# Window attention that divides by the softmax sum at the end instead of scaling the probabilities, with transfers that carry the sums and the halves of the result

## The chip, the cores and the metric

The kernel runs on 1 core of one Trainium2 chip. A core has a matrix engine (TensorE, PE in the profile; PEld are its weight loads), a vector engine (VectorE, DVE), an activation engine (ScalarE, ACT), a general engine (GpSimd, POOL) and an engine that issues transfers (SyncE, SP). Each runs its own list of instructions in order. They meet only at semaphores. The metric is the device time of one launch in microseconds (us). The time before is 2276.86 us, the median of 3 runs (2275.3 to 2279.8).

## The reference

The program is a trunk of two layers for 1024 tokens of width 1024, in float32. Layer 0 has two recurrences side by side (RG-LRU and HGRN2), layer 1 has windowed attention, and each is followed by a squared-ReLU MLP. Only the attention is touched. Its core is:

```python
q = rope(q.reshape(bsz, s, N_Q_HEADS, HEAD_DIM), cos, sin)       # 16 query heads of 64
k = rope(k.reshape(bsz, s, N_KV_HEADS, HEAD_DIM), cos, sin)      # 4 key heads, 4 query heads share one
sc = jnp.einsum('bnqhgd,bnkhd->bnhgqk', qb, kb).astype(jnp.float32) * (HEAD_DIM ** -0.5)
sc = jnp.where(band_mask[None, :, None, None], sc, -jnp.inf)     # +-128 tokens: blocks n-1, n, n+1
sink = jnp.broadcast_to(sinks..., sc.shape[:-1] + (1,))          # one more logit per head
p = jax.nn.softmax(jnp.concatenate([sc, sink], axis=-1), axis=-1)[..., :-1]
o = jnp.einsum('bnhgqk,bnkhd->bnqhgd', p.astype(vb.dtype), vb)
return o.reshape(bsz, s, N_Q_HEADS * HEAD_DIM) @ w_o
```

The sink is a logit that takes part in the softmax's maximum and sum and has no value row.

## The kernel before, in words

Matrix products keep float32 accuracy by splitting an operand into a rounded part (`hi`) and a rest (`lo`), each a matmul operand; `split` (L84 to L86) makes `hi` on ScalarE and `lo` on VectorE or, in the attention, for weights, on GpSimd.

The attention has two kinds of work. A **slab** is one projection of 128 output columns for half of the tokens: 24 matmuls (`proj`, L116), a copy out (L1074), four transfers that swap halves for the rotary positions (L1076), and rotary arithmetic on VectorE (L1077) and GpSimd (L1078, L1079). Weights of a slab come by one transfer of 512 KB into a tile with the tag `raw` (two buffers, L90) and are then split. A **unit** is one key head g (four query heads) and one block n of 128 queries; there are 32 units (`U00` to `U37`). A unit does this:

- for each of four heads, the scores: two matmuls (L1150, L1151), then one VectorE instruction that adds the mask, stores the 384 scores (256 at the ends) to `sm` and gives the row maximum `mx` (L1153);
- `nm`, the negative maximum with the sink (L1157), the sink's own exponential `es` (L1159, L1160), then four exponentials with their row sums `den` (L1163, ScalarE);
- `den` plus `es` (L1164), its reciprocal (L1165), and four VectorE instructions that scale the probabilities of a head by it (L1167);
- for each of 3 (or 2) key blocks: four transposes into one PSUM bank (L1172), the `hi`/`lo` split `ph`/`pl` (L85, L86), two matmuls with the values (L1177, L1178). The value operand holds `hi` in columns 0 to 63 and `lo` in 64 to 127, so the result `po` has two halves of 64 partitions that have to be added;
- the upper half is copied to `posb` (L1180, ScalarE) and four VectorE instructions add it to the lower half in PSUM and write 64x128 pieces of the result rows `ys` (L1183).

The order of slabs and units is written out in the string `ATT_ORDER`; a `!` marks a unit issued at high priority. A scheduler then merges all into one list per engine, by priorities, dependences and its own model of durations. So an edit in a unit moves the order of the whole stage. After the last unit the output projection (L216) multiplies `ys` by `w_o`, first for the rows of key heads 0 and 1, which may start while units run.

Of the kernel before, what the change touches and what calls it, by code (L numbers as in the profile page):

```python
# [18 lines left out]
P = 128  # L19
# [32 lines left out]
def trunk_kernel(ctx, tc, x, norm_g, rec_w_in, rec_conv_w, rec_conv_b, rg_w_r, rg_b_r, rg_w_i,  # L52
# [997 lines left out]
    def attention(xt, a):  # L1050
        w_qkv = att_w_qkv[a]
        ys = [yp.tile([P, S], F32, tag="y", name=f"y{i}") for i in range(KT)]
        with phase("att") as pool:
# [12 lines left out]

            def h512(name, bufs=2):
                return pool.tile([P, 512], F32, tag=name, name=name, bufs=bufs)
# [71 lines left out]
            def unit(g, n):  # L1140
# [4 lines left out]
                mx = pool.tile([P, GRP], F32, tag="mx", name="mx", bufs=2)  # L1145
                sm = []
                for j in range(GRP):
# [4 lines left out]
                    s_ = pool.tile([P, nk * P], F32, tag="sm", name="sm", bufs=8)  # L1152
                    V.tensor_tensor_reduce(out=s_, in0=o, in1=mask[:, mo:mo + nk * P], scale=1.0, scalar=-1e30,  # L1153
                                           op0=ALU.add, op1=ALU.max, accum_out=mx[:, j:j + 1])
                    sm.append(s_)
                nm = pool.tile([P, GRP], F32, tag="nm", name="nm", bufs=2)
                V.scalar_tensor_tensor(nm, mx, -0.125, nsink[:, g * GRP:(g + 1) * GRP], op0=ALU.mult, op1=ALU.min)  # L1157
                es = pool.tile([P, GRP], F32, tag="es", name="es", bufs=1)
                V.tensor_tensor(es, sink[:, g * GRP:(g + 1) * GRP], nm, op=ALU.add)  # L1159
                A.activation(es, es, AF.Exp)  # L1160
                den = pool.tile([P, GRP], F32, tag="den", name="den", bufs=2)
                for j in range(GRP):
                    A.activation(sm[j], sm[j], AF.Exp, scale=0.125, bias=nm[:, j:j + 1], accum_out=den[:, j:j + 1])  # L1163
                V.tensor_tensor(den, den, es, op=ALU.add)  # L1164
                V.reciprocal(den, den)  # L1165
                for j in range(GRP):
                    V.tensor_scalar(sm[j], sm[j], den[:, j:j + 1], None, op0=ALU.mult)  # L1167
                po = mm_ps("aux")
                for kc in range(nk):
                    pt = mm_ps("aux")  # L1170
                    for j in range(GRP):
                        T.transpose(pt[:, j * P:(j + 1) * P], sm[j][:, kc * P:(kc + 1) * P], ident)  # L1172
# [6 lines left out]
                ph_ = pool.tile([64, 512], F32, tag="po", name="posb", bufs=1)  # L1179
                A.activation(ph_, po[64:128, :], AF.Copy)  # L1180
                for j in range(GRP):
                    dst = ys[2 * g + j // 2][64 * (j % 2):64 * (j % 2) + 64, n * P:(n + 1) * P]
                    V.tensor_tensor(dst, po[0:64, j * P:(j + 1) * P], ph_[:, j * P:(j + 1) * P], op=ALU.add)  # L1183
# [114 lines left out]
```

## Time and profile before

| | |
|---|---|
| median of 3 runs | 2276.86 us (2275.3 to 2279.8) |
| the profiled execution, its own time | 2277.96 us |
| its span | 2276.3 us |
| TensorE busy | 2169.1 us, 95% of the span |
| VectorE busy | 1724.0 us, 76% |
| ScalarE busy | 1143.6 us, 50% |
| GpSimd busy | 251.0 us, 11% |
| scores of the first unit to values of the last | about 1247 to 1560 us of the span |

The share of an engine is an average over stages that have different limits; the attention is one of them, some 14% of the span. In the groups of the profile a row names line, engine, operation, output <- input, shape and count, then the busy time of the group and the mean duration of one. "Idle" behind the bar is the time in which the engine did nothing just before such an instruction, with what ended it.

### The profile page before, as it was taken

To read this page: it belongs to the slowest core of one execution; us is meant where nothing else is said; L and a number is where in the kernel's file an instruction comes from. 1 tells how busy PE (TensorE), PEld (TensorE's weight loads), DVE (VectorE), ACT (ScalarE), POOL (GpSimd) and SP (SyncE) were. 2 spreads that over 40 slices of the span, in tenths; PEclk is the share of its full clock that TensorE was granted. 3 is DMA by queue.
4 is the path that set the end of the run, shared out by engine and by line. 5 is a ranking of instruction groups with operands and counts; after the bars stand their busy time and mean duration, and the time that the engine had idled before them with its cause. 6 is when DMAs were issued, how large, how long until landed. Compare 5 with 4: busy or idle time off the path is not lost. (4 is left out here: it accounts for less than half of the span.)

```text
span 2276.3 us, 28192 instructions
## 1 busy us (share of the span) xinstructions
PE 2169.1 (95%) x10392; PEld 1785.3 (78%) x10392; DVE 1724.0 (76%) x2930; ACT 1143.6 (50%) x1812; POOL 251.0 (11%) x139
## 2 busy tenths in 40 slices
PE   7999999899899999999999888989899999999998
PEld 6878888687688888888888766668678888888886
DVE  6597766757966665678887888996986666578887
ACT  5576545445544445433434666775554445533342
POOL 1131000103000000000023244320300000000003
PEclk9999999999999999999999999999999999999999
DMA  5111001034344447444434111114444443644433
GB/s 140 51 33 56 29 29 37 28 104 148 120 166 153 153 144 254 153 139 150 138 124 141 46 38 44 40 38 139 139 138 151 152 152 135 249 139 153 153 117 129
DMA packets 180763, 264.03 MB, mean 116 GB/s; under 512 B 17040, under 2 KB 98960, under 8 KB 180624
## 3 DMA queue, kind: packets, MB, share of 16 engines
q1 hardware_dynamic: 180624, 262.22, 35.1%
q8 instruction: 82, 1.34, 0.2%
q14 instruction: 57, 0.47, 0.1%
HBM read 179.87 MB, written 70.78 MB: 110 GB/s over the span
## 5 line engine op out<-in xcount | busy, mean ns | idle before, releaser
L116 PE MATMUL m<-xh,w1hl 128*128 128x512 f32 (+1 forms) x1472 | 429.9, 371 | 0.2 <-ACT qf L1074 0.2
L116 PEld LDWEIGHTS m<-xh,w1hl 128*128 128x128 f32 x1472 | 266.9, 192 | 38.0 <-ACT qf L1074 0.4
L116 PE MATMUL m<-xl,w1hl 128*128 128x512 f32 (+1 forms) x736 | 274.0, 372 | 0.0
L236 POOL TENSOR_TENSOR mg<-acc,g 128x1024 f32<-128x1024 f32 x32 | 83.5, 2610 | 1447.3 <-DVE acc L553 1207.3
L86 DVE TENSOR_TENSOR w1hl<-raw,w1hl 128x1024 fp32r<-128x1024 f32 x105 | 132.1, 1260 | 100.0 <-ACT w1hl L85 99.7
L418 PE MATMUL aux<-xh,w1hl 128*128 128x512 f32 x512 | 168.3, 390 | 0.0
L418 PE MATMUL m<-xh,w1hl 128*128 128x512 f32 x512 | 168.0, 390 | 0.4 <-ACT xh L85 0.4
L418 PE MATMUL m<-xh,ws 128*128 128x512 f32 x512 | 167.8, 390 | 0.0
L567 ACT ACTIVATE hidh<-hidl 128x1536 fp32r<-128x1536 f32 (+1 forms) x56 | 89.4, 1597 | 147.9 <-DMA hidl<-hs 147.9
L644 PE MATMUL m<-w2h,hidh 128*128 128x512 f32 x416 | 161.8, 389 | 0.0
L644 PE MATMUL m<-w2l,hidh 128*128 128x512 f32 x416 | 161.8, 389 | 0.0
L644 PE MATMUL m<-w2h,hidl 128*128 128x512 f32 x416 | 161.8, 389 | 0.0
L116 PEld LDWEIGHTS m<-xl,w1hl 128*128 128x128 f32 x736 | 141.8, 193 | 19.1 <-DVE xl L205 0.2
L568 DVE TENSOR_TENSOR hidl<-hidl,hidh 128x1536 fp32r<-128x1536 f32 (+1 forms) x56 | 105.9, 1891 | 56.9 <-ACT hidh L567 56.9
L85 ACT ACTIVATE w1hl<-raw 128x1024 fp32r<-128x1024 f32 x116 | 122.2, 1055 | 32.0 <-PE m L418 11.0
L85 ACT ACTIVATE ws<-s 128x512 fp32r<-128x512 f32 x88 | 55.4, 632 | 145.2 <-PE m L418 88.0
L85 ACT ACTIVATE w2h<-b 128x1536 fp32r<-128x1536 f32 (+1 forms) x48 | 76.7, 1598 | 100.4 <-PE m L644 49.1
L644 PE MATMUL aux<-w2h,hidh 128*128 128x512 f32 x312 | 121.4, 389 | 0.0
L644 PE MATMUL aux<-w2l,hidh 128*128 128x512 f32 x312 | 121.4, 389 | 0.0
L644 PE MATMUL aux<-w2h,hidl 128*128 128x512 f32 x312 | 121.4, 389 | 0.0
L418 PEld LDWEIGHTS m<-xh,w1hl 128*128 128x128 f32 x512 | 96.2, 188 | 21.0 <-ACT xh L85 1.2
L418 PEld LDWEIGHTS m<-xh,ws 128*128 128x128 f32 x512 | 96.1, 188 | 20.9 <-ACT ws L85 0.6
(298 smaller groups left out, 5165.9 us busy)
## 6 DMA issues: line engine op xcount, KB each, us to landing
hidl<-hs SPq DMA_DIRECT2D x42, 768.0 KB, 4.6
raw<-in_mlp_w_dram SPq DMA_DIRECT2D x30, 1024.0 KB, 5.5
hs<-hid SPq DMA_DIRECT2D x104, 256.0 KB, 2.1
b<-in_mlp_w_dram SPq DMA_DIRECT2D x24, 768.0 KB, 4.8
raw<-in_rec_w_in_dram SPq DMA_DIRECT2D x28, 512.0 KB, 3.8
hidl<-hs SPq DMA_DIRECT2D x14, 1024.0 KB, 5.6
hs<-u SPq DMA_DIRECT2D x52, 256.0 KB, 2.0
hres<-hb SPq DMA_DIRECT2D x24, 512.0 KB, 3.1
```

Of the source, the lines that this page charges most:

```text
L85: A.activation(hi, src, AF.Copy)
L86: (eng or V).tensor_tensor(lo, src, hi, op=ALU.subtract)
L116: T.matmul(o[:, c0:c0 + nw], a[:, k, :], b[k // 4][half][:, k % 4, c0:c0 + nw], start=(n == 0), stop=(n == 3 * KT - 1))
L236: G.tensor_tensor(mg, m, g_post, op=ALU.mult)
L418: T.matmul(o, a[:, k, :], b[:, k, :], start=(first and n == 0), stop=(n == 11), skip_group_check=not first)
L567: A.activation(h, f32(l), AF.Copy)
L568: V.tensor_tensor(l, f32(l), h, op=ALU.subtract)
L644: T.matmul(o, a_[:, j, sl], b_[:, j, :], start=(not more and n == 0), stop=(n == last), skip_group_check=more)
```

## The change

- The probabilities are no longer scaled. The reciprocal sums `den` (128 queries x 4 heads) are stored to DRAM as 4 rows of 128 numbers, and each row is read back broadcast over 64 partitions, into `rd`.
- The result `po` is copied out whole (128 partitions). Two transfers move its halves to the other partitions (64 x 256 numbers each), so that heads of even number have their rest on partitions 0 to 63 and heads of odd number on 64 to 127. Two VectorE instructions (64x256) add, two (128x128) multiply by `rd` and write `ys`.
- The sink is column 0 of the score tile: GpSimd copies `nsink` there, the exponential covers one column more and its row sum holds the sink. Scores are stored times -0.125, the running minimum starts at `nsink`, so `nm`, `es` and the addition to `den` need no instructions of their own.
- The scratch tiles `x_` and `rd` (two sets) live in one of the two `raw` buffers for the whole attention. The score tile is one tile of four heads with two buffers, where there were eight of one head.

```diff
+            scr = wp.tile([P, 2, 2, 2, P], F32, tag="raw", name="scr")
+            scr = [(scr[:, i, 0], scr[:, i, 1]) for i in range(2)]
...
-                mx = pool.tile([P, GRP], F32, tag="mx", name="mx", bufs=2)
-                sm = []
+                nm = pool.tile([P, GRP], F32, tag="nm", name="nm", bufs=2)
+                sm = pool.tile([P, GRP, 3 * P + 1], F32, tag="sm", name="sm", bufs=2)
+                heads = slice(g * GRP, (g + 1) * GRP)
+                G.tensor_copy(sm[:, :, 0:1], nsink[:, heads].rearrange("p (j o) -> p j o", o=1))
                 for j in range(GRP):
...
-                    s_ = pool.tile([P, nk * P], F32, tag="sm", name="sm", bufs=8)
-                    V.tensor_tensor_reduce(out=s_, in0=o, in1=mask[:, mo:mo + nk * P], scale=1.0, scalar=-1e30,
-                                           op0=ALU.add, op1=ALU.max, accum_out=mx[:, j:j + 1])
-                    sm.append(s_)
-                nm = pool.tile([P, GRP], F32, tag="nm", name="nm", bufs=2)
-                V.scalar_tensor_tensor(nm, mx, -0.125, nsink[:, g * GRP:(g + 1) * GRP], op0=ALU.mult, op1=ALU.min)
-                es = pool.tile([P, GRP], F32, tag="es", name="es", bufs=1)
-                V.tensor_tensor(es, sink[:, g * GRP:(g + 1) * GRP], nm, op=ALU.add)
-                A.activation(es, es, AF.Exp)
+                    V.tensor_tensor_reduce(out=sm[:, j, 1:1 + nk * P], in0=o, in1=mask[:, mo:mo + nk * P], scale=-0.125,
+                                           scalar=nsink[:, g * GRP + j:g * GRP + j + 1], op0=ALU.add, op1=ALU.min,
+                                           accum_out=nm[:, j:j + 1])
                 den = pool.tile([P, GRP], F32, tag="den", name="den", bufs=2)
                 for j in range(GRP):
-                    A.activation(sm[j], sm[j], AF.Exp, scale=0.125, bias=nm[:, j:j + 1], accum_out=den[:, j:j + 1])
-                V.tensor_tensor(den, den, es, op=ALU.add)
+                    e_ = sm[:, j, 0:1 + nk * P]
+                    A.activation(e_, e_, AF.Exp, scale=-1.0, bias=nm[:, j:j + 1], accum_out=den[:, j:j + 1])
                 V.reciprocal(den, den)
-                for j in range(GRP):
-                    V.tensor_scalar(sm[j], sm[j], den[:, j:j + 1], None, op0=ALU.mult)
+                den_d = dr.tile([GRP, P], F32, name=f"den{a}_{g}{n}")
+                Y.dma_start(den_d.rearrange("j q -> q j"), den)
                 po = mm_ps("aux")
...
-                ph_ = pool.tile([64, 512], F32, tag="po", name="posb", bufs=1)
-                A.activation(ph_, po[64:128, :], AF.Copy)
-                for j in range(GRP):
-                    dst = ys[2 * g + j // 2][64 * (j % 2):64 * (j % 2) + 64, n * P:(n + 1) * P]
-                    V.tensor_tensor(dst, po[0:64, j * P:(j + 1) * P], ph_[:, j * P:(j + 1) * P], op=ALU.add)
+                t = h512("po", 1)
+                A.activation(t, po, AF.Copy)
+                t4 = t.rearrange("p (j e q) -> p j e q", j=2, e=2)
+                x_, rd = scr[n % 2]
+                for e in range(2):
+                    dst, src = slice(64 * e, 64 * e + 64), slice(64 - 64 * e, 128 - 64 * e)
+                    Y.dma_start(x_[dst], t4[src, :, e, :])
+                    Y.dma_start(rd[dst], den_d.rearrange("(j e) q -> e j q", e=2)[e].partition_broadcast(64))
+                    V.tensor_tensor(x_[dst], t4[dst, :, e, :], x_[dst], op=ALU.add)
+                for j in range(2):
+                    V.tensor_tensor(ys[2 * g + j][:, n * P:(n + 1) * P], x_[:, j], rd[:, j], op=ALU.mult)
```

The scheduler gives other lists on each engine from about the attention on. Three places follow. Lines of the changed kernel are shifted: L1157 there is the score instruction, L1163 the exponential, L1164 the reciprocal, L1166 the store of `den`, L1179 the copy of `po`, L1184 the transfers of its halves into `scr`, L1185 the reads of `den` into `scr`, L1186 and L1188 the additions and products, L1151 the copy of the sink. Names of waits are the engine, or one of eight counters of transfers, that a row waits for.

VectorE, the end of a unit's softmax in the second half of the attention, before:

```order
L1164 TENSOR_TENSOR den<-den,es 128x4 [waits Activation_49]
L86 TENSOR_TENSOR pl<-aux,ph 128x512 [waits Activation_49]
L1157 SCALAR_TENSOR_TENSOR nm<-mx,nsink 128x4 [waits DVE_49]
L1165 RECIPROCAL den<-den 128x4 [waits DVE_49]
L1183 TENSOR_TENSOR y_9689<-aux,posb 64x128
L1159 TENSOR_TENSOR es<-sink,nm 128x4 [waits DVE_49]
L1167 TENSOR_SCALAR sm<-sm,den 128x384 [waits DVE_49]
L1167 TENSOR_SCALAR sm<-sm,den 128x384 x3
```

and VectorE behind the reciprocal of one of the last units of key head 1, in the change:

```order
L1164 RECIPROCAL den<-den 128x4 [waits DMAHW5_49,Activation_49]
L86 TENSOR_TENSOR pl<-aux,ph 128x512 [waits Activation_49]
L1080 TENSOR_TENSOR qf<-qf,cos 128x512 [waits DMAHW6_49,DMAHW5_49,DMAHW7_49,DMAHW0_49,Pool_49]
L1186 TENSOR_TENSOR scr<-po,scr 64x256 [waits DMAHW1_49]
L86 TENSOR_TENSOR pl<-aux,ph 128x512 [waits Activation_49]
L1186 TENSOR_TENSOR scr<-po,scr 64x256 [waits DMAHW2_49]
L86 TENSOR_TENSOR pl<-aux,ph 128x512 [waits Activation_49]
L1188 TENSOR_TENSOR y_9684<-scr 128x128 [waits DVE_49]
```

The scaling between reciprocal and transposes is gone; additions that wait for a transfer now stand between the splits `pl`, for which TensorE waits.

SyncE while key head 0 is under way, before:

```order
L1076 DMA rot<-qf 32x512 [waits DMAHW0_49,DMAHW7_49,DVE_49,Activation_49]
L1076 DMA rot<-qf 32x512
L1076 DMA rot<-qf 32x512 [waits DMAHW1_49]
L1076 DMA rot<-qf 32x512 [waits DMAHW2_49]
L1076 DMA rot<-qf 32x512 [waits DMAHW4_49,DMAHW5_49,DMAHW3_49,DMAHW6_49,Activation_49,Pool_49]
```

and when key head 1 begins, in the change:

```order
L1079 DMA rot<-qf 32x512
L1166 DMA den_11_10893<-den 128x4x1 [waits DMAHW4_49,DVE_49]
L1166 DMA den_12_10964<-den 128x4x1 [waits DMAHW5_49,DVE_49]
L1079 DMA rot<-qf 32x512 [waits DMAHW6_49]
L1079 DMA rot<-qf 32x512 [waits DMAHW7_49]
L1185 DMA scr<-den_11_10893 64x2x128 [waits DMAHW4_49,DMAHW0_49]
L1185 DMA scr<-den_12_10964 64x2x128 [waits DMAHW5_49,DMAHW1_49]
L1185 DMA scr<-den_11_10893 64x2x128 [waits DMAHW2_49]
L1185 DMA scr<-den_12_10964 64x2x128 [waits DMAHW3_49]
L90 DMA raw<-in_att_w_qkv_dram 128x8x128 [waits Pool_49]
L1166 DMA den_10_11035<-den 128x4x1 [waits DVE_49]
L1184 DMA scr<-po 64x2x128 [waits DMAHW6_49,Activation_49]
```

The reads of `den` stand a few rows behind its store and wait for its landing (counters 4 and 5); the rotary transfers, a weight load and the next unit's halves share that queue.

GpSimd in the same stretch, before:

```order
L1078 TENSOR_TENSOR rot<-rot,sin 128x512 [waits DMAHW5_49,DMAHW6_49,DMAHW4_49,DMAHW3_49]
L1079 TENSOR_TENSOR qf<-qf,rot 128x512 [waits DVE_49,Pool_49]
L1106 TENSOR_TENSOR qst<-qf,qst 64x512 [waits Activation_49] x2
L86 TENSOR_TENSOR w1hl<-raw,w1hl 128x1024 [waits PE_49,Activation_49,Pool_49]
L1078 TENSOR_TENSOR rot<-rot,sin 128x512 [waits DMAHW2_49,DMAHW3_49,DMAHW1_49,DMAHW0_49]
```

and in the change:

```order
L86 TENSOR_TENSOR w1hl<-raw,w1hl 128x1024 [waits PE_49,DMAHW6_49,Activation_49,Pool_49]
L1151 COPY sm<-nsink 128x4 [waits DVE_49,PE_49]
L1081 TENSOR_TENSOR rot<-rot,sin 128x512 [waits DMAHW6_49,DMAHW7_49,DMAHW3_49,DMAHW2_49]
L1082 TENSOR_TENSOR qf<-qf,rot 128x512 [waits DVE_49,Pool_49]
L1151 COPY sm<-nsink 128x4 [waits PE_49]
L1109 TENSOR_TENSOR qst<-qf,qst 64x512 [waits Activation_49,Pool_49]
L1151 COPY sm<-nsink 128x4 [waits PE_49,Pool_49]
```

A unit's exponentials now wait for a copy that stands behind rotary work and weight splits on GpSimd.

More of the change, by code (lines that the diff above doesn't have):

```diff
@@ L1171, in unit @@
                     for j in range(GRP):
-                        T.transpose(pt[:, j * P:(j + 1) * P], sm[j][:, kc * P:(kc + 1) * P], ident)
+                        T.transpose(pt[:, j * P:(j + 1) * P], sm[:, j, 1 + kc * P:1 + (kc + 1) * P], ident)
                     ph = pool.tile([P, 512], F32R, tag="ph", name="ph", bufs=2)
```

## The prediction

> **What bounds the kernel now.** I read the page's shares and slices first, then the chain of waits, then busy times by stretch.
>
> ```profile
> span 2276.3 us, 28192 instructions
> PE 2169.1 (95%) x10392; PEld 1785.3 (78%) x10392; DVE 1724.0 (76%) x2930; ACT 1143.6 (50%) x1812; POOL 251.0 (11%) x139
> ```
>
> ```profile
> core 0: us, PE busy (x) PEld busy (x) DVE busy (x) ACT busy (x) POOL busy (x), PEclk, DMA share, GB/s
> 1247.00:1420.00 173.00, 151.54 (x735) 120.47 (x736) 148.89 (x389) 105.98 (x254) 67.27 (x45) 0.95 0.17 45
> 1420.00:1560.00 140.00, 127.84 (x633) 97.13 (x632) 125.39 (x380) 96.59 (x239) 35.07 (x22) 0.99 0.13 35
> 1700.00:1900.00 200.00, 200.00 (x884) 165.62 (x883) 137.02 (x193) 101.06 (x150) 0.00 (x0) 1.00 0.45 153
> ```
>
> TensorE sets the time. In the MLP (third row) it has no gap at all. In the two rows of the units it is idle for 21.5 + 12.2 = 33.6 us, and VectorE is busy for 86% and 90%. Its clock was 0.95 in the first; at 1.0 that row would hold up to 0.05 x 173 = 8.7 us less. A change inside the units can win these 42 us at most, by the visible gaps. What ends TensorE's gaps between 1225 and 1575 us is in its waits (total, times, longest):
>
> ```profile
> PE aux L1172 <- DVE sm L1167: 11.9, 13, 2.8
> PE aux L1178 <- DVE pl L86: 5.5, 6, 1.6
> PE m L1150 <- DVE mx L1153: 3.3, 5, 1.1
> PE aux L1172 <- DVE y L1183: 1.9, 1, 1.9
> ```
>
> These four are 22.6 us and all are VectorE. So the units are held by VectorE's queue, and most by the scaling of probabilities, which stands on the path from exponential to transpose.
>
> **What leaves VectorE.** Groups of the same stretch by shape:
>
> ```profile
> L86 DVE TENSOR_TENSOR pl<-aux,ph 128x512 fp32r<-128x512 f32 x88 | 59.4, 683 | 9.9 <-ACT ph L85 9.5
> L1167 DVE TENSOR_SCALAR sm<-sm,den 128x384 f32<-128x384 f32 x96 | 47.9, 549 | 0.4
> L1183 DVE TENSOR_TENSOR y<-aux,posb 64x128 f32<-64x128 f32 x128 | 35.9, 280 | 3.6 <-ACT posb L1180 2.0
> L1077 DVE TENSOR_TENSOR qf<-qf,cos 128x512 f32<-128x512 f32 x20 | 17.7, 885 | 1.8 <-DMA rot<-qf 1.7
> L1167 DVE TENSOR_SCALAR sm<-sm,den 128x256 f32<-128x256 f32 x32 | 13.7, 481 | 0.1
> L1159 DVE TENSOR_TENSOR es<-sink,nm 128x4 f32<-128x4 f32 x32 | 12.5, 390 | 0.3
> L1164 DVE TENSOR_TENSOR den<-den,es 128x4 f32<-128x4 f32 x32 | 9.3, 291 | 9.9 <-ACT sm L1163 9.4 <-ACT es L1160 0.3
> L1157 DVE SCALAR_TENSOR_TENSOR nm<-mx,nsink 128x4 f32<-128x4 f32 x32 | 9.1, 286 | 0.3
> ```
>
> Scaling 47.9 + 13.7, result pieces 35.9, the three small ones 12.5 + 9.3 + 9.1: 128.4 us go.
>
> **What comes to VectorE.** Per unit two additions 64x256 and two products 128x128, all from SBUF. The rows nearest are in the recurrence of layer 0:
>
> ```profile
> L900 DVE TENSOR_TENSOR lk<-q,sp 128x256 f32<-128x256 f32 x16 | 8.9, 557 | 0.0
> L903 DVE TENSOR_TENSOR lk<-km,g 128x256 f32<-128x256 f32 x16 | 6.7, 418 | 0.0
> L134 DVE TENSOR_TENSOR e<-y 128x4 f32<-128x4 f32 x8 | 1.3, 160 | 2.6 <-ACT y L804 2.6
> ```
>
> 64 additions at 418 ns are 26.8 us. A product of 128 columns lies between 160 and 418 ns; on the line through both it is 0.16 + 0.258 x 124/252 = 0.29 us, 64 of them 18.4 us. Together 45 us; at the dearer 557 ns and 418 ns they are 62 us. So VectorE is freed of 66 to 83 us; I take 77, or 2.4 us a unit. The score instruction keeps its shape, though its scale, its start value and its offset of one column are new. I price that at nothing; 50 ns on each of 128 would be 6 us of VectorE, well inside the relief.
>
> **The other engines.** The exponential of the sink leaves ScalarE, the copy of `po` doubles its partitions, each exponential has a column more:
>
> ```profile
> L1163 ACT ACTIVATE sm<-sm,nm 128x384 f32<-128x384 f32 x96 | 58.0, 605 | 20.3 <-DVE nm L1157 20.0
> L1180 ACT ACTIVATE posb<-aux 64x512 f32<-64x512 f32 x32 | 19.1, 596 | 5.2 <-PE aux L1178 4.0 <-DVE y L1183 0.2
> L1160 ACT ACTIVATE es<-es 128x4 f32<-128x4 f32 x32 | 6.2, 195 | 4.7 <-DVE es L1159 4.6
> L1074 ACT ACTIVATE qf<-m 128x512 f32<-128x512 f32 x19 | 11.3, 595 | 7.8 <-DVE qst L1106 3.5 <-issue 2.5 <-PE m L116 0.9
> ```
>
> 128 partitions cost what 64 do (595 against 596 ns), so ScalarE loses 6.2 us of work. TensorE's matmuls are the same in number and shape. GpSimd gets 32 copies of 128x4. Each lies between 0.16 us (VectorE's row for that shape) and the 1.46 us of a rotary product of 512 columns below: 5 to 47 us, of which I take 8, since the shape is that of the first. GpSimd is busy 102 of 313 us, so the copies matter by their place only: they stand behind `rot`, and the exponentials wait for them.
>
> ```profile
> L1078 POOL TENSOR_TENSOR rot<-rot,sin 128x512 f32<-128x512 f32 x20 | 29.2, 1462 | 86.4 <-DMA rot<-qf 54.4 <-DVE y L1183 15.9 <-DVE kl L1092 8.0
> L85 ACT ACTIVATE w1hl<-raw 128x1024 fp32r<-128x1024 f32 x12 | 12.7, 1059 | 2.6 <-PE m L116 2.4
> L86 POOL TENSOR_TENSOR w1hl<-raw,w1hl 128x1024 fp32r<-128x1024 f32 x8 | 19.1, 2382 | 24.2 <-ACT w1hl L85 20.1 <-PE m L116 3.9
> ```
>
> **The transfers.** Per unit: one store of `den`, two reads of it, two moves of halves; 160 more on SyncE. Issues by size with median time to landing, then SyncE's time for one issue (min/median/max), then two loads in pieces of 4 bytes at the start of the program:
>
> ```profile
> rot<-qf SPq DMA_DIRECT2D x64, 64.0 KB, 2.0
> raw<-in_att_w_qkv_dram SPq DMA_DIRECT2D x6, 512.0 KB, 3.8
> L1076 SPq DMA_DIRECT2D rot<-qf x80: 507/588/1503, 1224.9 to 1494.8; - x80
> conv_w<-in_rec_conv_w_dram SPq DMA_DIRECT2D x4, 2.0 KB, 2.3
> br<-in_rg_b_r_dram SPq DMA_DIRECT2D x2, 2.0 KB, 3.5
> ```
>
> SyncE has 160 x 0.59 = 94 us more to issue in 313 us beside the 70 shown and a few more; it has room, but the work comes in bursts. A half (64 KB) lands 2.0 us after its issue, the second is issued 0.59 us later, so the additions can start 3.2 us behind the copy of `po` if nothing stands ahead on SyncE. What is queued behind a waiting addition on VectorE is the next split `pl`, and TensorE waits for that. The store of `den` writes 512 pieces of 4 bytes. No row shows such a store; loads in such pieces land in 2.3 to 3.5 us. Until it has landed the read of `den` holds SyncE, and behind it rotary transfers, halves and weights. The product itself is no concern: reciprocal to product has transposes, splits, values and copy between, more than store plus read (3.5 + 2.0 us).
>
> Here a rule speaks against the change. The row says 2.0 us for 64 KB between SBUF addresses. The Trainium skill, "DMA: Bandwidth & Descriptors", section "Anatomy of one DMA — SWDGE (gpsimd) path", puts about 2.0 us of fixed cost on a transfer, mostly the receipt of the last write, and calls HBM the heaviest target, with surprisingly long delays. Its table "Specifications" adds that below 512 B an engine reads, modifies and writes. By the rows the store is 3.5 us at most; by the page it could be above, which is the case of the second rival. No run here shows it yet.
>
> **Weights.** `raw` has one buffer left, so loading does not overlap splitting: 3.8 us landing, 1.06 us on ScalarE and 2.38 on GpSimd, 7.2 us for the weights of two slabs. The chain of waits gives the pace of a bare matmul (start, us, what), and the page its drawn length:
>
> ```profile
> 1665.92 20.85 PE m L418 x92
> ```
>
> ```profile
> L418 PE MATMUL m<-xh,w1hl 128*128 128x512 f32 x512 | 168.0, 390 | 0.4 <-ACT xh L85 0.4
> ```
>
> 20.85/92 = 0.227 us, so the 48 matmuls of two slabs take 10.9 us and cover it. Without that cover (a load 5 us late behind waits on SyncE) six loads would cost 6 x (7.2 + 5 - 10.9) = 8 us. I take nothing.
>
> **The sum.** The waits for scaling and result pieces go entirely: 11.9 + 1.9 = 13.8 us. Of those for `pl` and the scores (8.8 us), which are a full queue, I let half go: 4.4. A wait shows short, since a matmul is drawn to its end, 0.39 us, where the next may start after 0.227; 0.16 us in each of 25 waits is 4 us. Gain 22 us. Against it stands what VectorE waits for transfers. How much of VectorE's time reaches TensorE is read from above: 61.6 us of scaling cost 11.9 us of wait (19%), 59.4 us of `pl` 5.5 (9%), 35.9 us of pieces 1.9 (5%). I take one fifth. The hold is bounded below by nothing (other work fills it) and above by 3.2 us a unit if no store is in the way. I take 1 us a unit, since the list places splits between: 32 x 1 x 0.2 = 6 us. Net -16 us: span 2260, own time 2277.96 - 16 = 2262, and as the profiled run stood 1.1 us over the median, 2261 us for the median.
>
> **Rivals.** *The units become dense.* If the freed 2.4 us a unit empties VectorE's queue, more of the 42 us goes; 30 to 50 us, with 38 as the middle: 2239 us. For it: ScalarE waited 20 us for `nm` alone. Also for it: weight loads, one for each matmul, fill 217.6 of 313 us in the units and 165.62 of 200 us in the gapless MLP, a density of 0.84, so some 50 us may be slack where the visible gaps say 42. Against it: ScalarE keeps 196 of its 202 us, and with less to do VectorE may only hand the wait on to it. The Trainium skill ("Trainium Kernel Development and Optimization", section "Performance Expectations") says the same of the two measures: matmul busy time misleads, weight-load share is the good one. By that rule alone the ceiling would be the 50 us, by the busy row 42.
>
> *The transfers eat it.* The hold is not 1 but about 3.4 us a unit (32 x 3.4 x 0.2 = 22): no change, 2277 us.
>
> *SyncE stops at the store.* Store (3.5 us), halves behind it (2.0) and an issue between (0.59) in series make 6.1 us a unit on VectorE: 32 x 6.1 x 0.2 = 39 us, less 22: +17, 2294 us. It decides from 3.4 us a unit on. For it: the read stands four rows behind its store, with rotary transfers between that GpSimd, and so the sink's copy and the exponentials, wait for. GpSimd already waits 54 us for those transfers. Against it: the list was laid out with transfers that take time.
>
> **How the numbers follow.** Forecast (gain 5 to 30 us) 0.47, dense 0.15, eaten 0.15, SyncE 0.23. This kernel's runs tell 0.2%, 4.6 us, from no change. So faster 0.62, same 0.15, slower 0.23. The forecast's own range is 2247 to 2272. For 8 in 10, the lower end lies at the dense case's middle (2238), leaving about 0.07; the upper at 2290, short of the last rival's middle, leaving about 0.12.
>
> **What would show it.** Right: in the unit stretch VectorE falls to about 65 to 70%, TensorE's waits on the scaling vanish, its idle falls from 33.6 to under 20 us, and VectorE's waits on `scr` are some 30 us in all. Steps wrong: additions 64x256 well over 0.42 us, or `den` landing above 3.5 us. The forecast is wrong if VectorE or ScalarE waits over 100 us for transfers, if exponentials wait on GpSimd's copy, or if slabs wait for `raw`.

## The result and the profile after

The changed kernel takes 2424.76 us (median of 4 runs, 2422.95 to 2425.02) against 2276.18 us (2275.3 to 2279.8) of the kernel before on the same chip: 1.0648 times as long, 95% interval 1.0635 to 1.066, or 149 us more. The forecast was 2261 us, its range ended at 2290: wrong in sign and size, and even the rival that ends above, 2294, holds only 17 of the 149 us.

The page of the changed kernel (span, busy times, granted clock in 40 slices):

```profile
span 2423.2 us, 28338 instructions
PE 2210.1 (91%) x10392; PEld 1821.1 (75%) x10392; DVE 1663.9 (69%) x2706; ACT 1142.1 (47%) x1780; POOL 256.9 (11%) x171
PEclk9999999999999999999997788788989999999999
```

VectorE did lose work: 1663.9 us where it had 1724.0. The slices of the units, and one behind them, show a lower clock; the kernel before has a 9 in every slice. The same 1376 or so matmuls stand in the first row below (kernel before) and in the second (after); the columns are stretch, length, busy time of TensorE, its weight loads, VectorE, ScalarE, GpSimd, then the granted clock, the busy share of the transfer engines and GB/s.

```profile
1247.00:1562.00 315.00, 281.38 (x1376) 219.14 (x1377) 274.89 (x770) 203.76 (x495) 102.34 (x67) 0.97 0.15 40
```

```profile
1247.00:1707.00 460.00, 318.97 (x1377) 252.15 (x1377) 217.55 (x549) 205.00 (x467) 109.54 (x97) 0.82 0.23 48
```

The units take 460 us in place of 315, 145 us more, which is nearly the whole loss. TensorE is idle for 141.0 us of them (33.6 before): 107.4 us of standing. The other 37.6 us is the same matmuls drawn longer, at a granted clock of 0.82 instead of 0.97; how much of it is the clock's, no run separates. Every engine but TensorE is busy for less than half of the stretch. So the time is waiting, and the transfers show for what (output and input, queue, operation, count, KB each, median us from issue to landing, 1240 to 1720 us):

```profile
rot<-qf SPq DMA_DIRECT2D x70, 64.0 KB, 2.4
scr<-den SPq DMA_DIRECT2D x64, 64.0 KB, 3.9
scr<-po SPq DMA_DIRECT2D x64, 64.0 KB, 4.5
den<-den SPq DMA_DIRECT2D x32, 2.0 KB, 9.8
```

The smallest transfer is the slowest. The store of 2 KB lands in 9.8 us, and a half of 64 KB in 4.5 us where the prediction had 2.0. The waits of the changed kernel in that stretch (total us, times, longest), then SyncE's own and TensorE's:

```profile
DVE scr L1186 <- DMA scr<-po: 108.9, 26, 13.4
POOL rot L1081 <- DMA rot<-qf: 74.0, 11, 12.3
ACT po L1179 <- DVE scr L1186: 69.5, 18, 8.6
DVE qf L1080 <- DMA rot<-qf: 34.3, 8, 8.6
ACT sm L1163 <- DMA den<-den: 25.3, 5, 8.2
```

```profile
SPq L1185 <- DMA den<-den: 91.8, 15, 11.2
```

```profile
PE aux L1176 <- ACT ph L85: 27.2, 9, 7.7
PE aux L1177 <- DVE pl L86: 26.1, 7, 5.1
PE m L1155 <- DVE nm L1157: 23.4, 6, 9.0
PE m L1155 <- POOL qst L1109: 12.5, 5, 5.9
```

VectorE stands for the halves, ScalarE for VectorE (the copy of `po` has one buffer, which the addition frees) and for the store itself (an exponential sums into a `den` whose last store must have left), GpSimd for rotary halves (74.0 us, against 49.5 in the kernel before), SyncE for the store. TensorE's waits name ScalarE, VectorE and GpSimd in turn: no one queue is full, all stand together. One such stop, from the timeline of the changed kernel (start, us, engine, line, and in brackets the idle time before and what ended it):

```profile
1506.51 0.55 SPq L1166 DMA_DIRECT2D den<-den  x1
...
1515.74 0.58 SPq L1185 DMA_DIRECT2D scr<-den  x1
...
1516.42 0.55 SPq L1166 DMA_DIRECT2D den<-den  x1
...
1517.69 1.26 SPq L1184 DMA_DIRECT2D scr<-po  x2
...
1526.91 0.87 DVE L1186 TENSOR_TENSOR scr<-po,scr 64x256 f32<-64x256 f32 x2 [13.45 <-DMA scr<-po]
1527.87 0.60 ACT L1179 ACTIVATE po<-aux 128x512 f32<-128x512 f32 x1 [8.56 <-DVE scr L1186]
...
1528.52 0.90 PE L1121 MATMUL aux<-ident,qf 128*128 128x128 f32 x3 [7.94 <-ACT po L1179]
```

A store goes out at 1506.51 and its read only at 1515.74, 9.2 us later. The next store goes out at 1516.42 and two halves behind it at 1517.69. These read nothing that the store writes, yet they arrive only at 1526.9, some 10 us after that store was issued. Then VectorE, ScalarE and TensorE move, one after the other. Were the transfer engines full meanwhile? The same stretch in two parts, in the columns of above:

```profile
1517.70:1520.10 2.40, 0.75 (x2) 0.50 (x2) 0.00 (x0) 1.60 (x5) 0.00 (x0) 0.58 0.56 110
1520.10:1526.90 6.80, 0.47 (x2) 0.00 (x0) 0.00 (x0) 0.00 (x0) 0.00 (x0) 0.50 0.00 0
```

They were not. By 1520.1 us all packets of these transfers have ended, and in the 6.8 us up to the landing no packet is on record at all. So what came late was not the halves' turn on the transfer engines but the report that they had landed: the store before them landed at 1526.5, they at 1526.9 and 1527.0. By the issue and landing times in the trace this is the rule in the unit stretch (1240 to 1720 us). Of the 76 transfers that SyncE issued while a store was still over 2.5 us from its landing, none landed before that store; all landed 0.2 to 4.8 us behind it. Of the 64 halves 33 were issued so and landed in 8.8 us (median), the other 31 in 2.1; of the rotary moves 14 in 7.6 us, the other 55 in 2.0.

From here stood theory T1: the store of 512 pieces of 4 bytes lands in some 10 us, holds SyncE at the read behind it, and delays the transfers issued after it. Against it T2: the moves of halves, with one buffer for the copied result, hold the units whatever the store does. T3: GpSimd's copy of the sink column, or the single weight buffer. T4: only SyncE's stop at the read counts.

### The profile page after: what moved, and what is told of

Same layout as the page of the kernel before. It is cut to its first block, busy times and chain, and to the rows that moved or that the text cites. A ratio compares the mean times of both kernels' runs of the same rounds, so it can differ in the third digit from the quotient of the medians.

```text
span 2423.2 us, 28338 instructions
## 1 busy us (share of the span) xinstructions
PE 2210.1 (91%) x10392; PEld 1821.1 (75%) x10392; DVE 1663.9 (69%) x2706; ACT 1142.1 (47%) x1780; POOL 256.9 (11%) x171
## 5 line engine op out<-in xcount | busy, mean ns | idle before, releaser
L116 PE MATMUL m<-xh,w1hl 128*128 128x512 f32 (+1 forms) x1472 | 435.4, 375 | 7.3 <-ACT qf L1077 6.6
L116 PEld LDWEIGHTS m<-xh,w1hl 128*128 128x128 f32 x1472 | 270.9, 195 | 49.5 <-ACT qf L1077 7.6
L418 PEld LDWEIGHTS m<-xh,w1hl 128*128 128x128 f32 x512 | 96.1, 188 | 21.1 <-ACT xh L85 1.3
```

What stands on the lines that cost most here:

```text
L116: T.matmul(o[:, c0:c0 + nw], a[:, k, :], b[k // 4][half][:, k % 4, c0:c0 + nw], start=(n == 0), stop=(n == 3 * KT - 1))
L418: T.matmul(o, a[:, k, :], b[:, k, :], start=(first and n == 0), stop=(n == 11), skip_group_check=not first)
```

## The experiments

All ratios are to the kernel before, beside it on the same chip; its median there lay between 2276.1 and 2277.1 us. a1, a2, a9, a10, a11, d1 and d3 leave out the right normalisation of 31 units.

| kernel | median us | ratio, 95% interval |
|---|---|---|
| the change | 2424.76 | 1.0648 (1.0635 to 1.066) |
| a1: store once | 2285.69 | 1.0038 (1.0025 to 1.0051) |
| a2: stores kept, not read | 2411.99 | 1.06 (1.0585 to 1.0616) |
| a6: no moves of halves | 2373.15 | 1.0419 (1.0402 to 1.0437) |
| a3: store in rows of 128 bytes | 2285.24 | 1.0035 (1.002 to 1.0049) |
| a9: unread store, pieces of 16 bytes | 2289.79 | 1.0052 (1.0032 to 1.0072) |
| a10: unread store, 4 bytes, 512 apart | 2286.48 | 1.0031 (1.0016 to 1.0046) |
| a11: the same, 8 to 64 bytes apart | 2291.48 | one run |
| a4: sink as score column alone | 2269.49 | 0.9962 (0.9949 to 0.9975) |
| b3: a4 with one weight buffer | 2270.58 | 0.997 (0.9958 to 0.9982) |
| b1: a4, copy on VectorE | 2283.73 | 1.0028 (1.0018 to 1.0038) |
| w3: a4 in another order | 2282.73 | 1.0023 (1.001 to 1.0036) |
| a5: sums by matmuls, halves moved | 2293.77 | 1.0073 (1.0058 to 1.0089) |
| a7: sums by matmuls, no transfers | 2287.92 | 1.0046 (1.0029 to 1.0063) |
| a8: a7, copy on VectorE | 2280.68 | 1.0014 (1.0005 to 1.0023) |
| d2: a8 with half the matmuls | 2276.76 | 1.0 (0.9991 to 1.001) |
| c1: a3, no moves, copy on VectorE | 2282.48 | 1.0022 (1.0013 to 1.0032) |
| d1: a8, sums spread once | 2269.52 | 0.9964 (0.9951 to 0.9978) |
| d3: d1, copy on GpSimd | 2270.37 | 0.9976 (0.9966 to 0.9985) |

### Is it the store, and by which way?

a1 stores the sums in the first unit only:

```diff
-                den_d = dr.tile([GRP, P], F32, name=f"den{a}_{g}{n}")
-                Y.dma_start(den_d.rearrange("j q -> q j"), den)
+                if "d" not in first:
+                    first["d"] = dr.tile([GRP, P], F32, name=f"den{a}_{g}{n}")
+                    Y.dma_start(first["d"].rearrange("j q -> q j"), den)
+                den_d = first["d"]
```

> The changed kernel, but the reciprocal sums are stored to DRAM in the first unit only, and every unit reads that one tile back: 31 of 32 stores go, all 64 reads and 64 moves of halves stay. It leaves out the right normalisation of the other 31 units. Theory T1 (the store of 512 pieces of 4 bytes lands in some 10 us, holds SyncE at the read behind it and delays the transfers issued after it; that is most of the 148 us): 2425 falls to 2270-2310, TensorE's waits in the units fall from about 135 to under 50 us, a move of halves lands in under 2.5 us instead of 4.5. Rival T2 (the moves of halves, with one buffer for the copied result, hold VectorE and ScalarE whatever the store does): stays at 2390 or more. Rival T3 (GpSimd's copy of the sink column, behind the rotary work, or the single weight buffer): stays at 2390 or more. T4 (only SyncE's stop at the read): as T1.

2285.69 us. 139 of the 149 us go with 31 stores of 2 KB. The moves and reads are all still there and now land nearly as priced (2.0 us):

```profile
rot<-qf SPq DMA_DIRECT2D x68, 64.0 KB, 2.0
scr<-den SPq DMA_DIRECT2D x64, 64.0 KB, 2.7
scr<-po SPq DMA_DIRECT2D x64, 64.0 KB, 2.1
...
den<-den SPq DMA_DIRECT2D x1, 2.0 KB, 10.7
```

The one store that is left took 10.7 us: it is slow by itself, not by a crowd of others. It also shows the delay of a stranger. The transfer of `kh`, which has nothing to do with the sums, was issued 1.2 us behind it and landed 9.8 us later (the median of the six `kh` is 2.3 us), though its packets ended 4.6 us after its issue; it landed 0.3 us after the store, and TensorE stood 7.7 us for it. T2 and T3 fall as the main cause.

a2 keeps all 32 stores and reads the first unit's tile only:

```diff
                 Y.dma_start(den_d.rearrange("j q -> q j"), den)
+                den_d = first.setdefault("d", den_d)
```

> The changed kernel with all 32 stores kept, but every unit reads the tile of the first unit, so no read waits for a store of its own unit. It leaves out the right normalisation of the other 31 units. T1 (the store also fills the transfer queues, so that halves, rotary halves and weights issued behind it land late): 2360-2420, a move of halves still lands in 4 us or more. T4 (only SyncE's stop at the read counts): 2270-2310 as in the kernel that stores once, halves land in under 2.5 us. T2 and T3: 2390 or more.

2411.99 us. No read waits for its unit's store any more, and only 13 us are won. T4 falls. In a2 the transfers land like this, and VectorE waits for halves as in the change (107.9 us). Of 93 transfers issued behind a store that was over 2.5 us from its landing, again none landed before it.

```profile
scr<-po SPq DMA_DIRECT2D x64, 64.0 KB, 5.0
...
den<-den SPq DMA_DIRECT2D x32, 2.0 KB, 9.9
```

```profile
DVE scr L1188 <- DMA scr<-po: 107.9, 26, 11.6
```

So the store costs the time mostly by what it does to the transfers issued behind it: with the stores there a half takes 5.0 us, without them 2.1. It does not do so by keeping the transfer engines busy, as the expectation has it: in the stop above they moved nothing for 6.8 us. A second way is in a2 too: ScalarE waits 28.1 us for the stores themselves, to write into `den` again. No run takes the two apart.

a6 leaves the store and undoes the moves (the upper half to `posb`, four additions from PSUM as before, then the products):

```diff
-                t = h512("po", 1)
-                A.activation(t, po, AF.Copy)
...
-                    Y.dma_start(x_[dst], t4[src, :, e, :])
...
+                ph_ = pool.tile([64, 512], F32, tag="po", name="posb", bufs=1)
+                A.activation(ph_, po[64:128, :], AF.Copy)
...
+                for j in range(GRP):
+                    V.tensor_tensor(x_[64 * (j % 2):64 * (j % 2) + 64, j // 2], po[0:64, j * P:(j + 1) * P],
+                                    ph_[:, j * P:(j + 1) * P], op=ALU.add)
```

> The changed kernel with the moves of halves undone: the upper half of the result is copied by ScalarE and four VectorE instructions add it from PSUM as before, into the scratch tile; the store, the reads and the two products stay. Nothing of the computation is left out. T1: the store still holds SyncE and what is behind it, but no addition waits for a transfer behind it any more; VectorE's 109 us of waits for halves go, the rotary transfers stay late: 2300-2370. T2: the halves were the cause, so 2260-2300. T3: 2390 or more.

2373.15 us, just above the range that T1 gave. A third of the loss (52 us) went through the halves; two thirds stay. The waits that are left in a6 name the rotary halves (GpSimd 65.4 us), the reads (VectorE 40.6 us) and the stores (ScalarE 19.9 us); no run separates these.

a3 changes the form of the store: VectorE transposes the sums in blocks of 32x32, and 128 pieces of 128 bytes are written. The reads become four a unit, of half the size; the rest stays.

```diff
-                V.reciprocal(den, den)
+                V.reciprocal(denp[:, 0:GRP], den)
...
-                Y.dma_start(den_d.rearrange("j q -> q j"), den)
+                V.transpose(dent, denp)
+                Y.dma_start(den_d, dent)
```

> The changed kernel with the reciprocal sums transposed on VectorE in blocks of 32x32 first (one instruction of 128x32 more in each unit) and stored in 128 pieces of 128 bytes instead of 512 of 4; four reads in place of two, in pieces of 128 bytes. Nothing of the computation is left out. T1: the store lands in 2-4 us and the time is 2280-2340. T2 and T3: 2390 or more, with two reads a unit more to issue it may even rise to 2450.

2285.24 us with twice as many reads, the same as with one store. Its stores, of eight times as many bytes, land in 2.3 us (median of 32), so what was wrong is the form of the store, not the idea of sending the sums through DRAM:

```profile
den<-dent SPq DMA_DIRECT2D x32, 16.0 KB, 2.3
```

### What makes the store slow?

Three kernels read the first unit's tile and add one store in each unit that nothing reads. a9 writes 128 pieces of 16 bytes, a10 the 512 pieces of 4 bytes 512 bytes apart, a11 8, 16, 32 or 64 bytes apart by unit.

```diff
+                den_q = dr.tile([P, GRP], F32, name=f"den{a}_{g}{n}")                    # a9
+                Y.dma_start(den_q, den)
...
+                den_w = dr.tile([GRP, P, 128], F32, name=f"den{a}_{g}{n}")               # a10
+                Y.dma_start(den_w[:, :, 0:1].rearrange("j q o -> q j o"), den.rearrange("p (j o) -> p j o", o=1))
...
+                step = (2, 4, 8, 16)[n % 4]                                              # a11, as a10 with P, step
```

> The kernel that stores once, and in every unit one more store of the sums that nothing reads, laid out with the four sums of a query side by side: 128 pieces of 16 bytes, where the change has 512 of 4. It leaves out the right normalisation of 31 units. If the number of pieces sets the landing: 2 + (9.9 - 2)/4 = 4 us, and the time 2285-2310. If it is writes that share a small stretch of DRAM which wait for each other (four queries of one head next to each other in the change): also less than 9.9, but then the store with the pieces far apart falls too. If any store in short pieces is slow: 9 us or more, 2390-2425.

> The kernel that stores once, and in every unit one more store of the sums that nothing reads, as 512 pieces of 4 bytes that lie 512 bytes apart in DRAM. It leaves out the right normalisation of 31 units. If the number of pieces sets the landing: 9-11 us and 2390-2425 as with all stores kept and not read (2412). If neighbours in DRAM wait for each other: 5 us or less and 2285-2320.

> The kernel that stores once, and in every unit one more store of the sums that nothing reads, in 512 pieces of 4 bytes whose distance in DRAM is 8, 16, 32 or 64 bytes, by the unit (8 units each). It leaves out the right normalisation of 31 units. At 4 bytes the landing was 9.8 us, at 512 bytes 2.0. If pieces wait for each other that share a stretch of 64 bytes or less, landings fall with the distance: about 6, 4, 3 and 2 us. If the stretch is 512 bytes: 7 us or more at each of the four.

The times (2290, 2286, 2291 us) are within 6 us of the kernel that stores once (2286). The landings in a10 are these; `den_first` is the change's own form, issued once in the same run:

```profile
den<-den SPq DMA_DIRECT2D x32, 2.0 KB, 2.0
...
den_first<-den SPq DMA_DIRECT2D x1, 2.0 KB, 10.5
```

Same number of pieces, same size, same queue: 10.5 us where the pieces are neighbours, 2.0 us where they lie 512 bytes apart. The number of pieces, which I had first blamed, is not the cause by itself. a11 gives the steps (`a` 8 bytes apart, `b` 16, `c` 32, `d` 64):

```profile
dena<-den SPq DMA_DIRECT2D x8, 2.0 KB, 4.4
denb<-den SPq DMA_DIRECT2D x8, 2.0 KB, 2.8
denc<-den SPq DMA_DIRECT2D x8, 2.0 KB, 2.2
dend<-den SPq DMA_DIRECT2D x8, 2.0 KB, 2.1
```

Over the 2.0 us of the far pieces the excess is 7.8 us at a distance of 4 bytes, then 2.4, 0.8, 0.2 and 0.1. It is gone by 32 to 64 bytes. That writes into one short stretch of DRAM wait for each other is a reading that fits these numbers; where in the chip they wait, no run here shows.

### Where is the gain that should be left without the store?

a1 and a3 are still 9 us above the kernel before, where the prediction had 16 below. a1 in the unit stretch:

```profile
1247.00:1562.00 315.00, 281.13 (x1379) 221.20 (x1379) 214.60 (x543) 198.50 (x465) 109.20 (x96) 0.96 0.26 68
```

VectorE is 60.3 us less busy (214.60 against 274.89) and TensorE's idle time is unchanged (33.9 against 33.6 us). The waits for scaling are gone, others have come (the second is the one behind the store that a1 keeps, so a1 itself still pays for a store):

```profile
PE m L1156 <- POOL qst L1109: 11.3, 6, 3.1
PE m L1156 <- DMA kh<-kh: 7.7, 1, 7.7
...
PE aux L1180 <- DVE pl L86: 6.6, 6, 2.1
```

The following kernels take the parts one by one. a4 is the kernel before with the sink's column alone (and the score tile and score instruction that go with it); b3 takes one weight buffer from it (it holds `posb`); b1 moves the sink's copy to VectorE.

```diff
+                G.tensor_copy(sm[:, :, 0:1], nsink[:, heads].rearrange("p (j o) -> p j o", o=1))   # a4; b1: V.tensor_copy
...
+            scr = wp.tile([P, 2, 512], F32, tag="raw", name="scr")                                # b3
...
-                ph_ = pool.tile([64, 512], F32, tag="po", name="posb", bufs=1)
+                ph_ = scr[0:64, 0]
```

> The kernel before with one part of the change alone: the sink as score column 0 (GpSimd copies it, scores stored times -0.125, minimum from the sink, one score tile of four heads with two buffers in place of eight of one head). Scaling, result pieces and two weight buffers stay; no transfer is added. Nothing of the computation is left out. T1 (the store is the cause): 31 us of small VectorE work go, 8 us come with the dearer score instruction: 2262-2280. T3 (the sink's copy stands on GpSimd behind a score tile that is not yet free, and rotary work behind it): 2285 or more. What is left without the store, +9 us, would then be this part's.

> The kernel with the sink as score column alone (2269.5), with one of the two weight buffers taken away: it holds the copied half of the result instead. Nothing of the computation is left out. If the single weight buffer takes part of the gain (load 3.8, ScalarE 1.06 and GpSimd 2.38 us no longer overlap): 2275-2285. If 48 matmuls of two slabs cover it, as the prediction took: 2266-2273.

> The kernel before with the sink as score column alone, its copy on VectorE in place of GpSimd. Nothing of the computation is left out. If the copy on GpSimd holds the query operands here as it did without added transfers (7 us): 2259-2265. If VectorE is the bound with the scaling still on it: 2268-2276.

2269.49, 2270.58 and 2283.73 us. The sink's column alone is 0.38% faster than the kernel before and beats both kernels. The single weight buffer costs nothing that can be measured. The copy's move to VectorE cost 14 us, against what T3 gives and outside both ranges.

a5, a7 and a8 spread the sums by matmuls, without DRAM; a7 and a8 also add the halves from PSUM as a6 does; a8 copies the sink on VectorE. d2 halves the number of matmuls (VectorE writes each reciprocal 64 times).

```diff
+                rd = mm_ps("aux")
+                for j in range(GRP):
+                    T.matmul(rd[64 * (j % 2):64 * (j % 2) + 64, (j // 2) * P:(j // 2 + 1) * P],
+                             den[:, j:j + 1].to_broadcast([P, 64]), ident, start=True, stop=True)
```

> The changed kernel with the reciprocal sums spread by four matmuls of TensorE a unit (the sums' column as the stationary operand, repeated 64 times, the identity as the moving one) into a PSUM bank in place of the store and the two reads; the moves of halves stay. Nothing of the computation is left out. T1: no store, so 2270-2305: as in the kernel that stores once (2286), less what 64 reads took of SyncE, plus 128 matmuls of 0.1-0.2 us (13-25 us). T2 (halves hold the units): 2310 or more.

> The changed kernel with no added transfer: reciprocal sums spread by four matmuls a unit, and halves added from PSUM as before into the scratch tile, then the two products. Unscaled probabilities and the sink's column stay. Nothing of the computation is left out. If relief of VectorE (some 58 us by the rows) is what the units lacked: 2250-2270 with the 13-25 us of matmuls. If VectorE's relief reaches TensorE in no part, and GpSimd's or the score tile's order holds the units instead: 2276-2300.

> As the kernel without added transfers, with the sink's copy on VectorE in place of GpSimd. Nothing of the computation is left out. T3 (the copy, waiting on GpSimd for a score tile, holds the rotary products and the query operands behind it): 5-20 us less than that kernel, GpSimd's 75 us of waits for the score tile go and TensorE no longer waits for query operands. Otherwise: within 4 us of that kernel, or above it by VectorE's 32 x 0.16 = 5 us.

> The kernel with no added transfer and the sink's copy on VectorE, with two matmuls a unit in place of four: VectorE writes the reciprocals repeated 64 times (128x256, some 0.25 us more a unit), and one matmul serves two heads. Nothing of the computation is left out. If the matmuls take the relief back: half of 31.5 us less than 2280.7, so 2262-2270. If not: 2276-2290.

2293.77, 2287.92, 2280.68 and 2276.76 us. None is faster than the kernel before; d2 equals it (2277.14 us beside it). The 128 matmuls are drawn 31.2 us in a8. c1 is a3 with a6's additions and the copy on VectorE:

> The change with three things altered together: sums stored in 128 pieces of 128 bytes, halves added from PSUM instead of moved, the sink's copy on VectorE. Nothing of the computation is left out. If the three are what kept the gain away (store 139 us, halves some 6 by the two kernels with matmuls, copy 7): the kernel with no added transfer and the copy on VectorE (2280.7) less its 128 matmuls (31.5 us busy, 128 x 2 x 0.123 as drawn) plus what four reads a unit cost: 2250-2268. If reads and the store in rows still hold VectorE or SyncE: 2272-2290.

2282.48 us, not the 2250 to 2268 of the sum of single effects but inside the other range, in which reads and store still hold. Whether they do, or these edits simply don't add up, c1 doesn't tell. d1 and d3 leave out the transport of the sums (matmuls in the first unit only, copied to a tile that every unit uses), with the sink's copy on VectorE and on GpSimd:

```diff
+                if "d" not in first:
+                    first["d"] = 1
...
+                    A.activation(rd, rp[:, 0:2 * P].rearrange("p (j q) -> p j q", j=2), AF.Copy)
```

> The kernel with no added transfer and the sink's copy on VectorE (2280.7), but the four matmuls that spread the reciprocal sums run in the first unit only and every unit multiplies by that tile. It leaves out the right normalisation of 31 units. If VectorE's relief does reach TensorE and what brings the sums to their place takes it away again: 2245-2257, i.e. the gain of 22 us that the prediction took, or more. If the relief reaches TensorE in no part: 2268-2281.

> The kernel with the sums spread in the first unit only and halves added from PSUM (2269.5), with the sink's copy back on GpSimd, where the change has it. It leaves out the right normalisation of 31 units. If the copy on GpSimd holds the query operands (TensorE waited 8.2 us for them in that kernel already): 2275-2280. If VectorE's 9.7 us of copies are what counts: 2258-2267. If neither: within 4 us.

2269.52 and 2270.37 us. With nothing at all to carry, unscaled probabilities gain 7.6 us over the kernel before, and nothing over a4, which still scales. TensorE is idle in the unit stretch (1247 to 1562 us) for 26.8 us in d1 and 27.0 in a4, against 33.6 before. The engine of the copy changes nothing here (+0.9), where it was -7 and +14 above. So the copy as a cause is not borne out in either direction. What all these edits share is that the scheduler lays out the units anew. w3 asks what that is worth: a4 with one unit's mark changed.

```diff
-             "!U07 U05 Q101 !U11 !U12 !U10 !U13 Q111 Q200 U14 Q210 !U17 !U15 U16 Q201 Q211 "
+             "!U07 !U05 Q101 !U11 !U12 !U10 !U13 Q111 Q200 U14 Q210 !U17 !U15 U16 Q201 Q211 "
```

> The kernel with the sink as score column alone (2269.5), with one unit of 32 (key head 0, block 5) marked for high priority: the same instructions in another order, from the middle of the units on. Nothing of the computation is left out. If the order that the scheduler happens to make is worth as much as these small edits: 4 us or more away, either side. If the differences between the kernels come from their instructions: within 4 us, 2265.5-2273.5.

2282.73 us, 13 us above a4 with the same instructions. One other order is worth as much as most of the differences between 2270 and 2294 us in this list, so these can't be put down to the parts. What made a4 fast is its instructions together with its order; that the sink's column gains in general is not shown.

## Why the prediction was wrong

**The step that failed first: "By the rows the store is 3.5 us at most".** The rows were loads in pieces of 4 bytes (2.3 to 3.5 us), and the prediction itself said that no row shows such a store. They bound a load. The store took 9.8 us. The Trainium skill, "DMA: Bandwidth & Descriptors", section "Anatomy of one DMA — SWDGE (gpsimd) path", which warns of surprisingly long delays at a write into HBM, pointed the right way, though it speaks of transfers that GpSimd issues, and SyncE issues all of these. Its fixed 2 us agrees with a10 (2.0 us, into the same DRAM): the other 7.8 us come from the neighbourhood of the pieces, which neither that section nor any row of before told.

**The step that would have kept it wrong: "I take one fifth", the share of VectorE's hold that reaches TensorE.** With 9.8 us for the store the prediction's own formula gives 32 x (9.8 + 2.0 + 0.59) x 0.2 = 79, less 22: 57 us, 2334, still 91 us short. The hold itself can be read now: VectorE stood 108.9 us for halves, 3.4 us a unit. By the fifth that is 22 us and no change at all; TensorE's idle time rose by 107.4 us. The fifth was read from VectorE's busy time, when other engines had work meanwhile. A late transfer stops ScalarE (69.5 us), GpSimd (74.0) and SyncE (91.8) as well. The sign that the prediction set for its being wrong, over 100 us of VectorE's waits for transfers, is there.

**SyncE stops at the store**, the rival: right place, wrong path. SyncE's stop is real (91.8 us of its time), but taking it away won 13 us. That transfers which don't depend on the store are reported late behind it was no step of any case, although the rival spoke of halves "behind it".

**The clock.** The prediction counted a clock of 1.0 as a possible gain of 8.7 us. It went the other way, to 0.82, and the matmuls were drawn 37.6 us longer. That a lower clock goes with a TensorE that stands often is seen here (0.82 with 141 us idle, 0.97 with 34); that the standing causes it was not tried.

**The waits for scaling and result pieces gone "entirely", half of those for `pl` and the scores, "A wait shows short": gain 22.** The relief of VectorE came: 60 of the forecast 77 us (11 of the other 17 went to dearer additions, products and score instructions, below), and in a1 it is 68% busy, as the prediction's test said. The waits for scaling went. But TensorE's idle time did not fall in a1, where 7.7 us of it still stand behind the one store, and with all transport left out (d1) it fell by 6.8 us and the gain was 7.6 us, a third of the 22. Most of the wait was handed on, to query operands (8.2 us in d1) and splits; how much of that is the order of the units, w3 leaves open. The prediction had named this against the dense rival ("VectorE may only hand the wait on") and not applied it to its own sum.

**Terms that held or nearly.** Groups of the changed kernel:

```profile
L1157 DVE CUSTOM_DVE_ANT_0 sm<-m,mask,nsink 128x384 f32<-128x384 f32 x96 | 57.4, 616 | 31.8 <-PE m L1156 28.5 <-PE aux L1171 2.7
L1186 DVE TENSOR_TENSOR scr<-po,scr 64x256 f32<-64x256 f32 x64 | 33.2, 518 | 109.8 <-DMA scr<-po 108.9
L1188 DVE TENSOR_TENSOR y<-scr 128x128 f32<-128x128 f32 x64 | 21.1, 367 | 1.4 <-DMA scr<-den 0.7 <-DVE scr L1186 0.4
L1179 ACT ACTIVATE po<-aux 128x512 f32<-128x512 f32 x32 | 19.0, 593 | 69.6 <-DVE scr L1186 69.5
L1151 POOL COPY sm<-nsink 128x4 f32<-128x4 f32 x30 | 6.6, 222 | 152.8 <-PE aux L1171 122.7 <-ACT ph L85 16.8 <-issue 13.2
```

Additions 33.2 and products 21.1 us make 54.3, between the 45 of the cheap end and the 62 of the dear one. The score instruction went from 554 to 616 ns, which the prediction priced at nothing: 128 x 0.062 = 8 us. With both, 128.4 - 54.3 - 8 = 66 us of relief should be left; the two pages show 60.1 (1724.0 - 1663.9), and the 6 us between stand in none of these rows. The copy of 128 partitions cost 593 ns as said, and GpSimd's copies 6.6 us where 8 were taken. The single weight buffer at nothing was right (b3: +1.1 us).

**The bounds.** The range was built from 0 to 6.1 us a unit. An operation that no row shows was bounded by rows of another kind, which made the upper end too low to matter. The bounds should have been open upwards, with SyncE's stop and what is issued behind the store priced by that end.

## What to carry to other kernels

A column of 4-byte results should not be stored to DRAM so that neighbouring partitions write neighbouring words: transpose it on chip first, or lay it out so that each partition writes its own 16 bytes or its own stretch, and look at the landing of the smallest transfers first when a kernel with new transfers is slow. A transfer that lands late can be paid for by all that is issued behind it, and by every engine that waits there together: here TensorE's idle time rose by as much as VectorE stood for the halves, where a fifth had been taken from busy times. Where a scheduler lays out the order anew with each edit, measure what an edit of the order alone is worth before a difference of that size is put down to the edit: here one unit's mark was worth 13 us.

## What was not expected of the hardware

- A store of 512 pieces of 4 bytes to DRAM landed in 9.8 us with the pieces 4 bytes apart, 4.4 at 8, 2.8 at 16, 2.2 at 32, 2.1 at 64 and 2.0 at 512 bytes. 128 pieces of 16 bytes next to each other landed in 1.6 us (a9, x32), 128 of 128 bytes in 2.3 us. Size and number of pieces mattered less than the distance; at the same 16 bytes, 512 pieces of 4 took 2.8 us and 128 of 16 took 1.6. By the Trainium skill, "DMA: Bandwidth & Descriptors", section "Specifications", an engine reads, modifies and writes below 512 bytes. It gives no price for that, and 4-byte pieces that lie far apart show none above a move of 64 KB (2.0 us against 2.0 to 2.1).
- In the kernels with such stores, the halves' moves of 64 KB between SBUF addresses landed 4.5 to 5.0 us after their issue (median) in place of 2.1, though they touch neither that DRAM nor that tile. In the stop shown above their packets had ended 6.8 us before, and no packet was on record from then on. None of 169 transfers issued behind a store still under way (76 in the change, 93 in a2) landed before that store. Halves and rotary moves issued at other times in the change landed in 2.1 and 2.0 us. Why a landing is reported only behind that of the earlier store, no run shows.
- One start value per partition in place of a constant, a scale of -0.125 with a minimum, and a column's offset in a larger tile came with 62 ns more in the score instruction (616 against 554 ns); which of them costs it was not tried.
